# A 64-expert mixture-of-experts kernel: one eighth of a one-block expert's second product as plain fp32, second-block transposes into other banks, one-pass ranks and routing table

## The chip, the cores and the metric

The kernel runs on one core of a Trainium2 chip. The metric is the device time of one execution in microseconds (us). Its engines are TensorE (PE; its weight loads are listed apart as PEld), VectorE (DVE), ScalarE (ACT), GpSimd (POOL) and SyncE (SP, which here only issues transfers). They run side by side and wait for each other through semaphores.

## The reference

One layer of a hybrid model over 2048 tokens of width 1024: a normed and modulated input goes through a spatial-gating branch and a gated linear-attention branch, whose merged output is added to the residual. Then a second norm and a mixture of experts:

```
hn2 = modulate(rmsnorm(h, g_norm2), sh2, sc2)
pg = softmax(t @ wrg + brg); p_top, g_idx = top_k(pg, 1)          # 8 groups
l_top, e_local = top_k(le[g_idx], 2)                              # 8 experts in each
gate = p_top * softmax(l_top)                                     # two experts per token
hblk = silu(xblk @ w1[e]) * (xblk @ w3[e])                        # [128,1024] @ [1024,512] twice
y    = hblk @ w2[e]                                               # [128,512] @ [512,1024]
out  = rmsnorm(h + g2 * segment_sum(y * gate), g_final)
```

Tokens are sorted by expert into blocks of 128. With these inputs 57 of the 64 experts fill one block and seven fill two.

## The kernel before

**Precision.** All products are to be as good as fp32. A matrix is split into a high part `hi`, rounded to the format fp32r, and a rest `lo`; `split_w` (lines 79 to 81) does it with one ACT copy (L80) and one DVE subtraction (L81). A product is then three fp32r matmuls (`mm3`, L84 to L86): hi by hi, hi by lo, lo by hi. Products of F32 operands are left to the engine's plain fp32, which the built program lists as one matmul and the trace as two instructions.

**Routing (phase D, up to line 1151).** A loop over sixteen tiles of 128 tokens, last tile first, mixes 48 large products per iteration (`pmx`, the output projection), the norm, the router's logits (`pl`) and, for a tile some iterations back, its routing: `g_route` picks the experts (one-hot `oh`, sum `ot`), `g_rank` ranks the tokens of an expert by a product with a triangle of ones (`prk`: one product with `ot`, one with the running counts `coh`), and builds `what` (token number and gate at the expert's column) and `at` (one-hot of the rank). `d_tab` adds four products at^T what into `slots`, the table of tokens and gates by rank and expert. After the loop the last two tiles go through without other work beside them, and DVE takes indices `idx` and gates `gate` from `slots`.

**Experts (from line 1160).** Each expert has twelve weight tiles of 128 x 1024 (eight for the first two products, four for the second), each two halves of 512 columns: 24 halves, 16 of `up` and 8 of `down`. SP loads tiles into a ring of 28; a load waits until its ring place has been read for the last time. `need` issues the split of a half LA = 4 halves ahead of its product, into a ring of eight pairs `wh`, `wl`. `block` runs over the halves of `up` (into the two `pa` banks) or `down` (into the two `py` banks). The order on each engine is that in which the code is written: `up(e+1)` comes ahead of `down(e)`, then `yevac` of `py` (DVE, two instructions L1218) and the scatter-add (POOL). Within `down`, at its fifth half, the next-but-one expert's rows are transposed (`xprep`, L1196, into `tpe`) and split (`xhe`, `xle`); at its seventh half the gated rows are transposed (`htr`, L1204, into `th`) for the next `down`; they are split (`hsplit`, L1208 and L1209) at the fifth half of the next `up`.

Whether an expert has a second block is known only at run time: `up` and `down` are each written twice, under If (two blocks) and Else (one), by `both`. In the two-block form `up` first transposes the second block's rows `xq` into `py`, runs its products three halves behind into `tpe`, and `down` runs the second block into `pa`, which DVE then evacuates inside the branch (L1218 on `pa`).

Of the kernel before, what the change touches and what calls it, by code (L numbers as in the profile page):

```python
# [8 lines left out]
F32 = mybir.dt.float32  # L9
F32R = mybir.dt.float32r  # L10
# [3 lines left out]
AF = mybir.ActivationFunctionType  # L14
# [3 lines left out]
P = 128  # L18
# [12 lines left out]
def kernel(ctx: ExitStack, tc: tile.TileContext, a: dict, out: bass.AP):  # L31
# [16 lines left out]
    def pt(tag, shape, name):  # L48
        return psp.tile(list(shape), F32, name=name, tag=tag, bufs=NB[tag])
# [29 lines left out]
    def split_w(raw, hi, lo):  # L79
        act.activation(hi, raw, AF.Copy)  # L80
        vec.tensor_tensor(lo, raw, hi.bitcast(F32), op=OP.subtract)  # L81
# [761 lines left out]
    p1s.close()  # L843


    coh = const.tile([P, NE], F32, name="coh")
    vec.memset(coh, 0.0)
    zero = const.tile([P, 1], F32, name="zero")
    vec.memset(zero, 0.0)
    es = ExitStack()  # L850
    wk = es.enter_context(tc.tile_pool(name="p1d", bufs=1))
    bc = [wk.tile([P, D], F32, name=f"bc{i}") for i in range(2)]
    wr = wk.tile([P, KD, G + NE], F32, name="wr")
    br = wk.tile([P, G + NE], F32, name="br")
# [92 lines left out]
    def g_route(ti, rs=None):  # L947
        L = wk.tile([P, G + NE], F32, name="L", tag="L", bufs=2)
        if rs is None:
            vec.tensor_tensor(L, PL[ti], br, op=OP.add)  # L950
            yield
        else:
            vec.scalar_tensor_tensor(L, PL[ti], rs, br2, op0=OP.mult, op1=OP.add)
            yield
        gm, gi, gif = sm("gm", 8), sm("gi", 8, U32), sm("gif")
        vec.max(gm, L[:, 0:8])
        yield
        vec.max_index(gi, gm, L[:, 0:8])
        yield
        vec.tensor_copy(gif, gi[:, 0:1])  # L960
        yield
        nm, se, eg = sm("nm"), sm("se"), sm("eg", 8)
        og, mk = sm("og", 8), wk.tile([P, G, EG], F32, name="mk", tag="mk", bufs=2)
        vec.tensor_scalar(og, iota[:, 0:8], gif, None, op0=OP.is_equal)
        yield
        vec.tensor_scalar(nm, gm[:, 0:1], -1.0, None, op0=OP.mult)
        yield
        act.activation(eg, L[:, 0:8], AF.Exp, bias=nm, accum_out=se)
        vec.tensor_tensor(mk, L[:, 8:72].rearrange("p (g e) -> p g e", g=G),
                          og[:, :, None].to_broadcast([P, G, EG]), op=OP.mult)  # L970
        yield
        le = sm("le", 8)
        vec.tensor_reduce(le, mk.rearrange("p g e -> p e g"), axis=AX.X, op=OP.add)
        yield
        m1, i1, f = sm("m1", 8), sm("i1", 8, U32), sm("f", 2)
        vec.max(m1, le)
        yield
        vec.max_index(i1, m1, le)
        yield
        vec.tensor_copy(f[:, 0:1], i1[:, 0:1])  # L980
        yield
        o1, le2 = sm("o1", 8), sm("le2", 8)
        vec.tensor_scalar(o1, iota[:, 0:8], f[:, 0:1], None, op0=OP.is_equal)
        yield
        vec.scalar_tensor_tensor(le2, o1, -3.0e38, le, op0=OP.mult, op1=OP.add)
        yield
        m2, i2 = sm("m2", 8), sm("i2", 8, U32)
        vec.max(m2, le2)
        yield
        vec.max_index(i2, m2, le2)  # L990
        yield
        vec.tensor_copy(f[:, 1:2], i2[:, 0:1])
        yield
        df, e2, ef = sm("df"), sm("e2"), sm("ef", 2)
        vec.tensor_tensor(df, m2[:, 0:1], m1[:, 0:1], op=OP.subtract)
        yield
        act.activation(e2, df, AF.Exp)
        vec.scalar_tensor_tensor(ef, gif.to_broadcast([P, 2]), 8.0, f, op0=OP.mult, op1=OP.add)
        yield
        oh = wk.tile([P, 2, NE], F32, name="oh", tag="oh", bufs=2)  # L1000
        vec.tensor_tensor(oh, iota[:, None, :].to_broadcast([P, 2, NE]), ef[:, :, None].to_broadcast([P, 2, NE]),
                          op=OP.is_equal)
        yield
        ot = wk.tile([P, NE], F32, name="ot", tag="ot", bufs=2)
        vec.tensor_tensor(ot, oh[:, 0], oh[:, 1], op=OP.add)
        yield
        RT[ti] = e2, se, ot, oh, ef

    def g_rank(ti, *more_):
        e2, se, ot, oh, ef = RT[ti]  # L1010
        dn = sm("dn")
        prk = pt("aux", [P, NE], "prk")
        pe.matmul(prk, low, ot, start=True, stop=False)
        for m in more_:
            pe.matmul(prk, ones, m, start=False, stop=False)
        pe.matmul(prk, ones, coh, start=False, stop=True)
        pair = const.tile([P, 2, 2], F32, name="pair", tag="pair", bufs=3)
        pool.tensor_copy(pair[:, :, 0], tok[:, ti:ti + 1].to_broadcast([P, 2]))
        what = wk.tile([P, 2, 2, NE], F32, name="what", tag="what", bufs=2)
        act.activation(what[:, :, 0], oh, AF.Copy, scale=tok1[:, ti:ti + 1])  # L1020
        vec.scalar_tensor_tensor(dn, e2, 1.0, se, op0=OP.add, op1=OP.mult)
        yield
        vec.reciprocal(pair[:, 0, 1:2], dn)
        yield
        vec.tensor_tensor(pair[:, 1, 1:2], pair[:, 0, 1:2], e2, op=OP.mult)
        yield
        for i in range(2):
            act.activation(what[:, i, 1], oh[:, i], AF.Copy, scale=pair[:, i, 1:2])
        rk, at = sm("rk", 2), wk.tile([P, 2, 2 * P], F32, name="at", tag="at", bufs=2)
        ri = const.tile([P, 2], I32, name="ri", tag="ri", bufs=3)  # L1030
        prod = wk.tile([P, 2, NE], F32, name="prod", tag="prod", bufs=2)
        vec.tensor_tensor(prod, oh, prk[:, None, :].to_broadcast([P, 2, NE]), op=OP.mult)
        yield
        vec.tensor_tensor(coh, coh, ot, op=OP.add)
        yield
        vec.tensor_reduce(rk, prod, axis=AX.X, op=OP.add)
        yield
        for i in range(2):
            vec.tensor_scalar(at[:, i], pos, rk[:, i:i + 1], None, op0=OP.is_equal)
            yield  # L1040
        vec.scalar_tensor_tensor(ri, ef, float(S), rk, op0=OP.mult, op1=OP.add)
        yield
        SC[ti], TB[ti] = (ri, pair), (at, what)
# [32 lines left out]
    for it in range(NT):  # L1076
# [1 line left out]
        if it > 1:  # L1078
            d_x(ti)
        if it == 2:  # L1080
            slots = pt("mm", [P, 2, 2, NE], "slots")
            vec.memset(slots, 0.0)
        if it == 1:
            d_split(ti - 1)
# [62 lines left out]
    none = wk.tile([P, 2, NE], F32, name="none")  # L1147
    vec.tensor_scalar(none, slots[:, :, 0], 0.0, off, op0=OP.is_equal, op1=OP.mult)
    vec.scalar_tensor_tensor(idx.rearrange("p (b e) -> p b e", b=2), slots[:, :, 0], -1.0, none, op0=OP.add, op1=OP.add)
    vec.tensor_copy(gate.rearrange("p (b e) -> p b e", b=2), slots[:, :, 1])  # L1150
    es.close()


# [20 lines left out]
    PA, TP, PY, TH = ([psp.tile([P, 512], F32, name=f"{n}{i}") for i in range(2)] for n in ("pa", "tpe", "py", "th"))  # L1174
    four = lambda t: t.rearrange("p (c n) -> p c n", c=4)
    pc = TH[1][:, 0:NE]
    pe.matmul(pc, ones, coh, start=True, stop=True)
    ci_ = wk.tile([1, NE], I32, name="ci_")
    vec.tensor_scalar(ci_, pc[0:1], float(P - 1), None, op0=OP.add)
    vec.tensor_scalar(nblk, ci_, 7, None, op0=OP.logical_shift_right)  # L1180
# [4 lines left out]
    xhl = [wk.tile([P, KD, P], F32R, name=n) for n in ("xhe", "xle")]  # L1185
    hx = [wk.tile([P, KF, P], F32R, name=n) for n in ("hhe", "hle")]
    hx2 = [wk.tile([P, KF, P], F32R, name=n) for n in ("hh2", "hl2")]
    sh = wk.tile([P, F], F32, name="she")
    sh2 = [wk.tile([P, F], F32, name=f"sh2{i}") for i in range(2)]
    y1 = wk.tile([P, D], F32, name="y1")  # L1190
# [15 lines left out]
    def hsplit(th, hx):  # L1206
        hh, hl = hx
        act.activation(hh, four(th), AF.Copy)  # L1208
        vec.tensor_tensor(hl, four(th), hh.bitcast(F32), op=OP.subtract)  # L1209

    def glu(pa, sh):
# [18 lines left out]
    hpos = {v: p for p, v in enumerate(hseq)}  # L1230
    nsp = 0

    def need(p):
        nonlocal nsp
        while nsp <= min(p, len(hseq) - 1):
            e, k, i = hseq[nsp]
            split_w(W[e, k][:, i * 512:(i + 1) * 512], *ring[nsp % R])
            nsp += 1

    def both(two, one):  # L1240
# [13 lines left out]

        return [t.rearrange("p (k n) -> p k n", k=KD) for t in (xgr[e % 3], xqr[e % 2])]

    def block(base, n, outs, hls, at):

        for q in range(n + (LAG if len(outs) > 1 else 0)):
            if q < n:  # L1260
                need(base + q + LA)
                if q in at:
                    at[q]()
            for j, (o, hl) in enumerate(zip(outs, hls)):
                p = q - j * LAG
                if 0 <= p < n:
                    mms(o[p % 2], hl, p // 2, p % 2, n // 2, ring[(base + p) % R])

    def more(e):
# [44 lines left out]
    def up(e):  # L1314

        at = {4: lambda: hsplit(TH[0], hx)} if e else {}
        base = hpos[e, 0, 0]

        def two():
            xprep(xq[e % 2], rows2(e), PY)  # L1320
            block(base, 2 * KD, (PA, TP), (xhl, rows2(e)), at)
            glu(PA, sh)
            glu(TP, sh2[e % 2])

        def one():
            block(base, 2 * KD, (PA,), (xhl,), at)
            glu(PA, sh)

        g = both(two, one)
        with tc.If(NB_[e] > 1, preferred_fallthrough_block=False) as f:  # L1330
            next(g)
        with f.Else():
            next(g, None)

    def down(e):
# [13 lines left out]
            scat(y2, col(idx, NE + e))  # L1349

        def one():
            block(base, 2 * KF, (PY,), (hx,), at)

        g = both(two, one)
        with tc.If(NB_[e] > 1, preferred_fallthrough_block=False) as f:
# [119 lines left out]
```

## Time and profile before

| | us |
|---|---|
| three runs: lowest, median, highest | 2403.30, 2412.09, 2412.42 |
| profiled execution, its own time | 2410.06 |
| its span | 2408.4 |
| PE busy in the span | 2259.7 (94%) |
| DVE busy | 1932.1 (80%) |
| ACT busy | 1437.3 (60%) |
| POOL busy | 739.2 (31%) |

The profiled execution's time lies 2.0 us below the median of the runs. The mean granted clock is 0.969. Phase D spans about 780 to 1030 us, the experts about 1030 to 2330 us. A busy share averages over stages with different limits, so the views below are read stage by stage. A matmul's duration overlaps the next one's: what a product costs is the distance between starts.

### The profile page before, as it was taken

The page shows a single profiled execution, that of the slowest core. Times are in us where ns is not written, and L with a number is a line of the kernel's source. Part 1 is how long each engine was busy: PE and PEld are TensorE (multiplying, and loading weights), DVE is VectorE, ACT ScalarE, POOL GpSimd, SP SyncE. Part 2 cuts the span into 40 slices and gives each one's busy share as a digit, 9 for nine tenths or more (in the row PEclk, how much of TensorE's full clock was granted, in tenths as well). Part 3 has the DMA queues.
Part 4 walks back from the last instruction along what each step waited for, and adds up shares of the span by engine and source line. Part 5 has one row for each costly group of instructions (what it writes and reads, how often), then busy time and mean ns, then how long its engine had stood idle before and what let it go on. Part 6 is the DMA issues. An engine that isn't in the chain of part 4 may idle for free.

```text
span 2408.4 us, 40084 instructions
## 1 busy us (share of the span) xinstructions
PE 2259.7 (94%) x11932; PEld 1860.0 (77%) x11932; DVE 1932.1 (80%) x4302; ACT 1437.3 (60%) x2731; POOL 739.2 (31%) x602
## 2 busy tenths in 40 slices
PE   8999999989999899899999999999999999999990
PEld 3888888977777788778777888888777788888870
DVE  4556665657786888789887899999686699999986
ACT  3544444432332222378676788888575688888873
POOL 1123311146673122237431222323131132322220
PEclk9899999989999999989999999999999999999995
DMA  7333322356675654589997899999996799999947
GB/s 274 105 107 106 121 92 97 109 170 210 219 241 175 227 210 159 184 323 374 323 310 259 292 377 372 365 352 348 325 327 194 223 360 373 368 358 363 360 140 296
DMA packets 193220, 613.42 MB, mean 255 GB/s; under 512 B 36557, under 2 KB 36685, under 8 KB 192854
## 3 DMA queue, kind: packets, MB, share of 16 engines
q1 hardware_dynamic: 152358, 516.56, 59.0%
q0 software_dynamic: 38048, 87.95, 12.4%
q10 hardware_dynamic: 2448, 4.46, 0.5%
q8 instruction: 178, 2.92, 0.5%
q14 instruction: 188, 1.54, 0.2%
HBM read 547.42 MB, written 102.28 MB: 270 GB/s over the span
## 4 chain that ended last, share of the span: by engine, by line
PE 35%; DVE 11%; DMA 6%; issue 5%; ACT 1%; DVEq 0%; another core or an unknown queue 0%; SPq 0%; POOLq 0%; ACTq 0%; POOL 0%
DVE wl L81 9%; PE pa L84 7%; PE pa L86 7%; PE pa L85 7%; DMA we<-in_w_e_dram 3%; PE py L84 2%; PE py L85 2%; PE py L86 2%; DMA accD<-y,idx 2%; PE tpe L1196 1%; PE tpe L85 1%; PE tpe L84 1%; PE tpe L86 1%; DVE y L1218 1%; ACT wh L80 1%
## 5 line engine op out<-in xcount | busy, mean ns | idle before, releaser
L81 DVE TENSOR_TENSOR wl<-we,wh 128x512 fp32r<-128x512 f32 x1536 | 967.6, 732 | 82.5 <-ACT wh L80 76.2
L80 ACT ACTIVATE wh<-we 128x512 fp32r<-128x512 f32 x1536 | 892.9, 630 | 146.3 <-DVE wl L81 46.3
L84 PE MATMUL pa<-wh,xhe 128*128 128x512 f32 x1024 | 404.2, 395 | 9.5 <-ACT wh L80 7.5
L1221 POOL DMA_INDIRECT accD<-y,idx x71 | 245.7, 3460 | 525.0 <-DVE y L1218 440.5
L86 PE MATMUL pa<-wh,xle 128*128 128x512 f32 x1024 | 400.4, 391 | 0.0
L85 PE MATMUL pa<-wl,xhe 128*128 128x512 f32 x1024 | 399.9, 391 | 0.0
L84 PEld LDWEIGHTS pa<-wh,xhe 128*128 128x128 f32 x1024 | 192.6, 188 | 69.9 <-issue 28.6
L86 PEld LDWEIGHTS pa<-wh,xle 128*128 128x128 f32 x1024 | 192.6, 188 | 41.0
L1163 POOL DMA_INDIRECT xg<-hnD,idx x64 | 96.5, 1508 | 410.7 <-DVE wl L81 124.9
L85 PEld LDWEIGHTS pa<-wl,xhe 128*128 128x128 f32 x1024 | 192.8, 188 | 37.6
L84 PE MATMUL py<-wh,hhe 128*128 128x512 f32 x512 | 213.5, 417 | 6.7 <-ACT wh L80 6.2
L86 PE MATMUL py<-wh,hle 128*128 128x512 f32 x512 | 202.7, 396 | 1.5 <-issue 1.3
L85 PE MATMUL py<-wl,hhe 128*128 128x512 f32 x512 | 201.1, 393 | 2.9 <-DVE wl L81 2.9
L86 PEld LDWEIGHTS py<-wh,hle 128*128 128x128 f32 x512 | 97.0, 190 | 25.3 <-issue 3.1
L351 POOL TENSOR_SCALAR sc<-sc,dec 64x128 f32<-64x128 f32 x140 | 111.1, 793 | 17.8 <-PE po L683 6.4
L84 PEld LDWEIGHTS py<-wh,hhe 128*128 128x128 f32 x512 | 97.4, 190 | 24.5 <-issue 6.1
L85 PEld LDWEIGHTS py<-wl,hhe 128*128 128x128 f32 x512 | 97.7, 191 | 16.0
L1071 POOL DMA_INDIRECT tabD<-pair,ri x32 | 70.0, 2189 | 91.4 <-DMA tabD<-pair,ri 59.0
L1218 DVE SCALAR_TENSOR_TENSOR y<-py,gate,g2b 128x512 f32<-128x512 f32 x128 | 93.0, 791 | 4.0 <-PE py L86 3.9
L86 PE MATMUL pmx<-hi,mld 128*128 128x512 f32 x224 | 89.0, 397 | 6.1 <-DVE mld L81 6.1
L84 PE MATMUL pmx<-hi,mhd 128*128 128x512 f32 x224 | 91.9, 410 | 1.7 <-ACT mhd L80 1.7
L85 PE MATMUL pmx<-lo,mhd 128*128 128x512 f32 x224 | 88.0, 393 | 0.0
(417 smaller groups left out, 4651.2 us busy)
## 6 DMA issues: line engine op xcount, KB each, us to landing
we<-in_w_e_dram SPq DMA_DIRECT2D x765, 512.0 KB, 9.9
wt<-in_w_modB_dram SPq DMA_DIRECT2D x32, 512.0 KB, 5.7
kve<-kveD SPq DMA_DIRECT2D x48, 256.0 KB, 5.5
wt<-in_w_modA_dram SPq DMA_DIRECT2D x16, 512.0 KB, 7.5
x<-in_x_dram SPq DMA_DIRECT2D x16, 512.0 KB, 3.8
xD<-xf POOLq DMA_DIRECT2D x32, 256.0 KB, 3.1
mfd<-mxD SPq DMA_DIRECT2D x16, 512.0 KB
xd<-in_x_dram SPq DMA_DIRECT2D x16, 512.0 KB, 5.0
```

Source lines behind the costliest of these rows:

```text
L80: act.activation(hi, raw, AF.Copy)
L81: vec.tensor_tensor(lo, raw, hi.bitcast(F32), op=OP.subtract)
L84: pe.matmul(o, lh, wh, start=start, stop=False)
L85: pe.matmul(o, lh, wl, start=False, stop=False)
L86: pe.matmul(o, ll, wh, start=False, stop=stop)
L351: pool.tensor_scalar(s1[64:128, hs], s0[64:128, hs], dec[64:128, ci, h:h + 1], None, op0=OP.mult)
L1071: pool.indirect_dma_start(out=tabD, out_offset=bass.IndirectOffsetOnAxis(ap=ri[:, i:i + 1], axis=0), in_=pair[:, i], in_offset=None)
L1163: pool.indirect_dma_start(out=x, out_offset=None, in_=hnD, in_offset=bass.IndirectOffsetOnAxis(ap=ix, axis=0), bounds_check=S - 1, oob_is_ ...
L1196: pe.transpose(four(tp[c // 4])[:, c % 4], x[:, c * P:(c + 1) * P], ident)
L1218: vec.scalar_tensor_tensor(y[:, c], py[i], gt, g2b[:, c], op0=OP.mult, op1=OP.mult)
L1221: pool.indirect_dma_start(out=accD, out_offset=bass.IndirectOffsetOnAxis(ap=ix, axis=0), in_=y, in_offset=None, bounds_check=S - 1, oob_is ...
```

## The change

1. **Routing.** `ot`, `coh`, `what`, `at` and the two constant matrices (copied into `lor`) become fp32r, so `prk` and the table are single fp32r matmuls. Ones, token numbers and ranks are whole numbers; the gate is not, and is carried as `gh` + `gl` in two columns: `what` and `slots` grow from 2 to 3 x 64 columns, DVE adds the two after the loop.
2. **Second block.** `xprep` of the second block's rows goes into `tpe` instead of `py`.
3. **One-block `down`.** The last of its eight halves (position `raw`) is not split. Its product is one plain fp32 matmul of the raw weight half with `hf`, an unsplit copy of the last 128 columns of the gated rows, which ACT makes beside `hhe` in the space of a constant no longer used. The two-block form keeps all splits.

```diff
+    lor = wk.tile([P, 2, P], F32R, name="lor")
+    vec.tensor_copy(lor.rearrange("p t c -> p (t c)"), cst[:, 5 * P:7 * P])
+    lowr, onesr = lor[:, 0], lor[:, 1]
...
-        pe.matmul(prk, low, ot, start=True, stop=False)
+        pe.matmul(prk, lowr, ot, start=True, stop=False)
...
-        what = wk.tile([P, 2, 2, NE], F32, name="what", tag="what", bufs=2)
+        what = wk.tile([P, 2, 3, NE], F32R, name="what", tag="what", bufs=2)
...
+        gh, gl = wk.tile([P, 2], F32R, name="gh", tag="gh", bufs=2), sm("gl", 2)
+        act.activation(gh, pair[:, :, 1], AF.Copy)
+        vec.tensor_tensor(gl, pair[:, :, 1], gh.bitcast(F32), op=OP.subtract)
+        yield
         for i in range(2):
-            act.activation(what[:, i, 1], oh[:, i], AF.Copy, scale=pair[:, i, 1:2])
-        rk, at = sm("rk", 2), wk.tile([P, 2, 2 * P], F32, name="at", tag="at", bufs=2)
+            act.activation(what[:, i, 1], oh[:, i], AF.Copy, scale=gh[:, i:i + 1].bitcast(F32))
+            act.activation(what[:, i, 2], oh[:, i], AF.Copy, scale=gl[:, i:i + 1])
+        rk, at = sm("rk", 2), wk.tile([P, 2, 2 * P], F32R, name="at", tag="at", bufs=2)
...
-    vec.tensor_copy(gate.rearrange("p (b e) -> p b e", b=2), slots[:, :, 1])
+    ghi = wk.tile([P, 2, NE], F32, name="ghi")
+    vec.tensor_copy(ghi, slots[:, :, 1])
+    vec.tensor_tensor(gate.rearrange("p (b e) -> p b e", b=2), ghi, slots[:, :, 2], op=OP.add)
...
+    hf = tri_f
...
         act.activation(hh, four(th), AF.Copy)
+        if th is TH[0]:
+            act.activation(hf, four(th)[:, KF - 1], AF.Copy)
...
-            split_w(W[e, k][:, i * 512:(i + 1) * 512], *ring[nsp % R])
+            if nsp != raw:
+                split_w(W[e, k][:, i * 512:(i + 1) * 512], *ring[nsp % R])
             nsp += 1
...
-                if 0 <= p < n:
+                if base + p == raw:
+                    e, k, i = hseq[raw]
+                    pe.matmul(o[i], hf, W[e, k][:, i * 512:(i + 1) * 512], start=False, stop=True)
+                elif 0 <= p < n:
                     mms(o[p % 2], hl, p // 2, p % 2, n // 2, ring[(base + p) % R])
...
-            xprep(xq[e % 2], rows2(e), PY)
+            xprep(xq[e % 2], rows2(e), TP)
...
-            block(base, 2 * KF, (PY,), (hx,), at)
+            block(base, 2 * KF, (PY,), (hx,), at, base + 2 * KF - 1)
```

PE, the end of `down` in its one-block form, before (`py` and `th` are banks, `wh`/`wl` the split half, `she` the gated rows; the branch ends the form):

```order
L1204 MATMUL th_11188<-cst,she 128x128 x4
L84 MATMUL py_11186<-wh_11219,hhe 128x512
L85 MATMUL py_11186<-wl_11220,hhe 128x512
L86 MATMUL py_11186<-wh_11219,hle 128x512
L84 MATMUL py_11187<-wh_11221,hhe 128x512
L85 MATMUL py_11187<-wl_11222,hhe 128x512
L86 MATMUL py_11187<-wh_11221,hle 128x512
L1355 UNCONDITIONAL_BRANCH
```

and now (`cst` holds `hf`, `we` is the raw tile):

```order
L1216 MATMUL th_11288<-cst,she 128x128 x4
L84 MATMUL py_11286<-wh_11319,hhe 128x512
L85 MATMUL py_11286<-wl_11320,hhe 128x512
L86 MATMUL py_11286<-wh_11319,hle 128x512
L1283 MATMUL py_11287<-we_11234,cst 128x512
L1373 UNCONDITIONAL_BRANCH
```

One instruction (two in a trace) stands where three stood; nothing else on PE moves there. DVE in the same form, before:

```order
L81 TENSOR_TENSOR wl_11220<-we_11136,wh_11219 128x512
L81 TENSOR_TENSOR wl_11222<-we_11136,wh_11221 128x512
L81 TENSOR_TENSOR wl_11208<-we_11138,wh_11207 128x512
L1200 TENSOR_TENSOR xle<-tpe_11184,xhe 128x512
L1200 TENSOR_TENSOR xle<-tpe_11185,xhe 128x512
L81 TENSOR_TENSOR wl_11210<-we_11138,wh_11209 128x512
L81 TENSOR_TENSOR wl_11212<-we_11140,wh_11211 128x512
L81 TENSOR_TENSOR wl_11214<-we_11140,wh_11213 128x512
L1355 UNCONDITIONAL_BRANCH
```

and now:

```order
L81 TENSOR_TENSOR wl_11320<-we_11234,wh_11319 128x512
L81 TENSOR_TENSOR wl_11308<-we_11236,wh_11307 128x512
L1212 TENSOR_TENSOR xle<-tpe_11284,xhe 128x512
L1212 TENSOR_TENSOR xle<-tpe_11285,xhe 128x512
L81 TENSOR_TENSOR wl_11310<-we_11236,wh_11309 128x512
L81 TENSOR_TENSOR wl_11312<-we_11238,wh_11311 128x512
L81 TENSOR_TENSOR wl_11314<-we_11238,wh_11313 128x512
L1373 UNCONDITIONAL_BRANCH
```

The split of the last half (`wl_11222` before) is gone; the splits of the next `up` move one place forward. The routing loop on PE, as the difference of two places in one iteration:

```order
-L1013 MATMUL prk<-ot,cst 128x64
-L1016 MATMUL prk<-coh,cst 128x64
+L1017 MATMUL prk<-ot,lor 128x64
+L1020 MATMUL prk<-coh,lor 128x64
-L1064 MATMUL slots<-what,at 128x128 x4
+L1073 MATMUL slots<-what,at 128x192 x4
```

The places in the order stay; the products are now of fp32r operands and the table's are 192 columns wide.

## Rows read from the trace of the kernel before

**Rows 1.** Busy time by stretch: from and to, length, then busy time and instructions of PE, PEld, DVE, ACT and POOL, granted clock, share of the DMA engines, GB/s. The first stretch holds one-block experts alone, the second the routing loop.

```profile
1378.00:1687.00 309.00, 305.19 (x1428) 248.89 (x1427) 309.00 (x512) 267.72 (x474) 91.98 (x35) 1.00 0.99 363
830.00:1003.00 173.00, 173.00 (x971) 149.49 (x971) 141.53 (x569) 49.78 (x125) 45.12 (x59) 1.00 0.46 169
```

**Rows 2.** The timeline around the end of one `down` in that stretch: start, duration, engine, line, output and inputs, count, and in brackets idle time before it.

```profile
1499.21 3.17 DVE L81 TENSOR_TENSOR wl<-we,wh 128x512 fp32r<-128x512 f32 x5
...
1500.51 1.03 PE L1196 MATMUL tpe<-cst,xg 128*128 128x128 f32 x8
...
1501.30 0.47 PE L84 MATMUL py<-wh,hhe 128*128 128x512 f32 x1
...
1504.12 0.39 PE L85 MATMUL py<-wl,hhe 128*128 128x512 f32 x1
...
1504.35 0.40 PE L86 MATMUL py<-wh,hle 128*128 128x512 f32 x1
...
1504.89 0.19 PEld L84 LDWEIGHTS pa<-wh,xhe 128*128 128x128 f32 x1 [0.58 <-issue]
1504.92 0.47 PE L84 MATMUL pa<-wh,xhe 128*128 128x512 f32 x1 [0.18 <-ACT wh L80]
...
1505.23 1.48 DVE L1218 SCALAR_TENSOR_TENSOR y<-py,gate,g2b 128x512 f32<-128x512 f32 x2
1505.23 0.39 PE L85 MATMUL pa<-wl,xhe 128*128 128x512 f32 x1
```

**Rows 3.** The same place one expert later.

```profile
1522.47 0.40 PE L86 MATMUL py<-wh,hle 128*128 128x512 f32 x1
...
1523.09 0.47 PE L84 MATMUL pa<-wh,xhe 128*128 128x512 f32 x1 [0.22 <-ACT wh L80]
...
1523.37 1.49 DVE L1218 SCALAR_TENSOR_TENSOR y<-py,gate,g2b 128x512 f32<-128x512 f32 x2
```

**Rows 4.** The timeline of DVE, the last split ahead of the y at 1505.23.

```profile
1504.63 0.75 DVE L81 TENSOR_TENSOR wl<-we,wh 128x512 fp32r<-128x512 f32 x1
```

**Rows 5.** Waits of PE's weight loads over the expert stage (1030 to 2330): waiting group, releaser, us in total, times, longest.

```profile
PEld pa L84 <- issue: 28.6, 48, 0.7
```

**Rows 6.** The timeline of PE in the routing stage, plain fp32 products of 512 columns (L740: two products, four instructions) and what follows.

```profile
838.96 1.88 PE L740 MATMUL pm<-macc,cst 128*128 128x512 f32 x4
...
840.28 0.80 PE L84 MATMUL pmx<-hi,mhd 128*128 128x512 f32 x1
...
840.91 0.40 PE L85 MATMUL pmx<-lo,mhd 128*128 128x512 f32 x1
```

**Rows 7.** Groups of PE instructions over the expert stage: busy us, mean ns of one, idle us before them and what ended it. All transposes of second blocks.

```profile
L1196 PE MATMUL py<-cst,xq 128*128 128x128 f32 x56 | 9.0, 284 | 9.6 <-issue 7.5 <-DVE y L1218 2.2
```

**Rows 8.** The timeline at the head of one two-block `up`.

```profile
1248.01 0.40 PE L86 MATMUL py<-wh,hle 128*128 128x512 f32 x1
1249.04 1.41 DVE L1218 SCALAR_TENSOR_TENSOR y<-py,gate,g2b 128x512 f32<-128x512 f32 x2
...
1249.90 1.27 PE L1196 MATMUL py<-cst,xq 128*128 128x128 f32 x8 [1.49 <-issue]
...
1250.92 0.48 PE L84 MATMUL pa<-wh,xhe 128*128 128x512 f32 x1
```

**Rows 9.** The timeline of PE in one iteration of the routing loop.

```profile
891.25 0.33 PE L1013 MATMUL prk<-ot,cst 128*128 128x64 f32 x2
891.41 0.39 PE L1016 MATMUL prk<-coh,cst 128*128 128x64 f32 x2
891.63 1.96 PE L945 MATMUL pl<-wr,ht 128*128 128x72 f32 x16
...
898.99 1.06 PE L1064 MATMUL slots<-what,at 128*128 128x128 f32 x8
899.88 1.04 PE L934 MATMUL tpd<-cst,hn 128*128 128x128 f32 x8
...
906.26 0.33 PE L1013 MATMUL prk<-ot,cst 128*128 128x64 f32 x2
```

**Rows 10.** Groups of the routing loop (830 to 1003): the ACT instruction that writes a gate column of `what`, and the one-column DVE product beside it.

```profile
L1028 ACT ACTIVATE what<-oh,pair 128x64 f32<-128x64 f32 x24 | 7.1, 341 | 70.6 <-DVE pair L1023 70.6
...
L1025 DVE TENSOR_TENSOR pair<-pair,e 128x1 f32<-128x1 f32 x12 | 1.9, 159 | 0.4
```

**Rows 11.** The timeline after the loop: the first and the last products of the ranks of the last two tiles, their table, and DVE's first read of it.

```profile
1018.57 0.69 PE L1013 MATMUL prk<-ot,cst 128*128 128x64 f32 x2 [4.75 <-DVE ot L1005]
...
1020.33 0.63 PE L1016 MATMUL prk<-coh,cst 128*128 128x64 f32 x2
...
1022.48 3.75 PE L1064 MATMUL slots<-what,at 128*128 128x128 f32 x16 [1.51 <-DVE at L1039]
...
1026.27 0.35 DVE L1148 TENSOR_SCALAR none<-slots,off 128x128 f32<-128x128 f32 x1 [3.01 <-PE slots L1064]
```

**Rows 12.** The DMA view of 1380 to 1680 (all traffic; the weight loads, their KB and median us from issue to landing) and SP's waits there.

```profile
DMA packets 32746, 109.03 MB, mean 363 GB/s; under 512 B 6268, under 2 KB 6268, under 8 KB 32677
...
we<-in_w_e_dram SPq DMA_DIRECT2D x192, 512.0 KB, 11.3
...
SPq L613 <- DMA we<-in_w_e_dram: 117.5, 109, 3.1
SPq L613 <- DVE wl L81: 99.7, 120, 2.0
```

More of the change, by code (lines that the diff above doesn't have):

```diff
@@ L843 @@
     p1s.close()
-    coh = const.tile([P, NE], F32, name="coh")
-    vec.memset(coh, 0.0)
+    coh = const.tile([P, NE], F32R, name="coh")
+    cohf = coh.bitcast(F32)
+    vec.tensor_scalar(coh, cst[:, 0:NE], 0.0, None, op0=OP.mult)
     zero = const.tile([P, 1], F32, name="zero")
@@ L1003, in g_route @@
         yield
-        ot = wk.tile([P, NE], F32, name="ot", tag="ot", bufs=2)
+        ot = wk.tile([P, NE], F32R, name="ot", tag="ot", bufs=2)
         vec.tensor_tensor(ot, oh[:, 0], oh[:, 1], op=OP.add)
@@ L1012, in g_rank @@
         prk = pt("aux", [P, NE], "prk")
-        pe.matmul(prk, low, ot, start=True, stop=False)
+        pe.matmul(prk, lowr, ot, start=True, stop=False)
         for m in more_:
-            pe.matmul(prk, ones, m, start=False, stop=False)
-        pe.matmul(prk, ones, coh, start=False, stop=True)
+            pe.matmul(prk, onesr, m, start=False, stop=False)
+        pe.matmul(prk, onesr, coh, start=False, stop=True)
         pair = const.tile([P, 2, 2], F32, name="pair", tag="pair", bufs=3)
         pool.tensor_copy(pair[:, :, 0], tok[:, ti:ti + 1].to_broadcast([P, 2]))
-        what = wk.tile([P, 2, 2, NE], F32, name="what", tag="what", bufs=2)
+        what = wk.tile([P, 2, 3, NE], F32R, name="what", tag="what", bufs=2)
         act.activation(what[:, :, 0], oh, AF.Copy, scale=tok1[:, ti:ti + 1])
@@ L1033, in g_rank @@
         yield
-        vec.tensor_tensor(coh, coh, ot, op=OP.add)
+        vec.tensor_tensor(coh, cohf, ot.bitcast(F32), op=OP.add)
         yield
@@ L1080 @@
         if it == 2:
-            slots = pt("mm", [P, 2, 2, NE], "slots")
+            slots = pt("mm", [P, 2, 3, NE], "slots")
             vec.memset(slots, 0.0)
@@ L1176 @@
     pc = TH[1][:, 0:NE]
-    pe.matmul(pc, ones, coh, start=True, stop=True)
+    pe.matmul(pc, ones, cohf, start=True, stop=True)
     ci_ = wk.tile([1, NE], I32, name="ci_")
@@ L1231, with need @@
     nsp = 0
-    def need(p):
+    def need(p, raw=None):
         nonlocal nsp
@@ L1255, in rows2, with block @@
         return [t.rearrange("p (k n) -> p k n", k=KD) for t in (xgr[e % 3], xqr[e % 2])]
-    def block(base, n, outs, hls, at):
+    def block(base, n, outs, hls, at, raw=None):
         for q in range(n + (LAG if len(outs) > 1 else 0)):
             if q < n:
-                need(base + q + LA)
+                need(base + q + LA, raw)
                 if q in at:
```

## The prediction

> **What bounds the kernel now.** I read busy time by stretch first, since the change touches stages with different limits. In a stretch of one-block experts DVE is busy for all of its 309.00 us, in 512 instructions, so one every 0.604 us; PE is busy for 305.19 us [rows 1]. The timeline gives the period: one y starts at 1505.23, the next at 1523.37, 18.14 us later [rows 2, 3]. In it DVE has 30 instructions (24 weight splits, two xle, one hle, one she, two y), and 30 x 0.604 = 18.1. So DVE bounds a one-block expert, although PE's bar looks as full.
>
> The timeline also shows where PE gives the difference back. Products of the same kind start 0.23 us apart (1504.12, 1504.35). At the head of the next up the step is 0.57 (1504.35 to 1504.92), and one expert later 0.62 (1522.47 to 1523.09) [rows 2, 3]. The step behind it is 0.31 (1504.92 to 1505.23) in place of 0.23: a refill. The profile calls the wait "issue". The row of DVE says more: its last split began at 1504.63, so the one ahead of it, 0.604 earlier, with its duration of 0.75, ended at 1504.78, and PE's weight load begins at 1504.89 [rows 2, 4]. I read the gap as a wait for DVE: PE's first write to a pa bank waits on DVE's count, which in the one-block form has to reach the same place as in the two-block form, where DVE reads pa behind its last splits. PE alone would need 18.14 - 0.37 - 0.08, on average of the stops: **17.70 us**. The waits count 48 such stops over the expert stage [rows 5]; going through them in the timeline I put 41 behind one-block experts. In the rest DVE is not full.
>
> The routing loop is the opposite: PE is busy for 173.00 of 173.00 us and DVE for 141.53 [rows 1], at one iteration per 15.01 us (891.25 to 906.26) [rows 9]. What PE is spared there is gained.
>
> **One-block experts.** The change takes one split of 0.604 from DVE and one from ACT, which is not full (267.72 of 309.00) [rows 1]. DVE then has 29 instructions, 29 x 0.604 = 17.5 us. ACT gets a small copy instead; at most 0.34, the duration of a smaller one in routing [rows 10], it is under the split it replaces. On PE three fp32r steps of 0.23, 0.68 in all, become one plain fp32 product. The trace has such products of 512 columns: from the first of four L740 instructions (838.96) to the second product behind them (840.91) it takes 1.95 us, less the one fp32r step of 0.23 is 1.72 for two, **0.86 each**, entering and leaving fp32 included [rows 6]. That adds 0.18. An upper bound is one refill more, 0.08 as behind the present stop, so 0.26; below 0.86 nothing in the trace points. PE's period becomes 17.70 + 0.18 = 17.88, above DVE's 17.5: PE is now the bound, with DVE 0.3 to 0.4 us ahead of it per expert, which is what keeps the stop from coming back. The sum: 41 stops of 0.45 go, **-18.5**; 57 one-block experts pay 0.18, **+10.2** (bounds +10 to +15).
>
> [...]
>
> What is queued behind: the raw half is read by PE and no longer by DVE. DVE's fourth split from 1499.21 was the one of this half, over by about 1501.8; a product in its place on PE ends at about 1504.8 [rows 2]. So one of twelve weight tiles comes free 3 us later, and SP, which issues in order, holds back what stands behind it. A load takes 11.3 us from issue to landing at one per 1.56 us (192 in 300 us) [rows 12], so some seven are on their way and the bus stays fed: nothing.
>
> **Second blocks.** The eight transposes of second rows wait for DVE's y on py, the bank that they write. In one case y starts at 1249.04 and lasts to 1250.45; the transposes begin 1.89 us after the last product (1248.01 to 1249.90) in place of 0.23, and take 1.02 us to the next product in place of the 0.79 that undisturbed ones take (1500.51 to 1501.30) [rows 2, 8]. That is 1.66 + 0.23 = 1.89 us. The seven cases show PE idle for 9.6 us [rows 7]. Idle time counts from a product's end, 0.17 behind the start that the next would have had (a duration of 0.40 at steps of 0.23), so 7 x 0.17 = 1.2 come on top, and 7 x 0.23 = 1.6 for the slower transposes: 12.4. Bank tpe was last read by DVE's xle, two in a row behind the five splits from 1499.21 in an ordinary down and over before its last product, so the moved transposes find it free. What is late next would be xq: y ends at 1250.45, the first xq split, no longer than the 0.75 of a weight split [rows 4], by 1251.2. The next up would start at 1248.01 + 0.23 + 0.79 = 1249.03, and its products with xq four halves of 0.69 later, at 1251.8: in time. **-12.4** (bounds -9.6 to -12.5).
>
> **Routing loop.** Ranks take 0.38 us (891.25 to 891.63), the table 0.89 for eight instructions, 0.11 each (898.99 to 899.88) [rows 9]. The trace of before has no fp32r product below 256 columns. From below, the nearest row is an instruction of the table: 0.11 us, with its weight load. Four such make the table 0.45, two make the ranks 0.22: 0.60 per iteration. From above, plain fp32's rate: 192 of 512 columns of 0.86 is 0.32, four make 1.29, and the ranks stay as they are: 0.40 more. I take the lower price, since fp32r products of 512 columns here run at 0.23, so the format itself costs one pass. DVE and ACT get more work per tile: gl 0.16, a wait of one ACT step (0.34) ahead of it, and on ACT three more instructions of 0.34 [rows 10]; both have room (DVE 31 us, ACT 123 us idle in 173) [rows 1], and the table's product comes 7 us behind the ranks. Twelve iterations: **-7.3** (bounds -8 to +5).
>
> **Tail and setup.** After the loop the ranks and the table of the last two tiles stand on the path: DVE waits 3.01 us for the table [rows 11]. Eight rank instructions take 1.76 us (1018.57 to 1020.33), 0.22 each; ten become five, -1.1. Sixteen table instructions in 3.75 become eight, -1.9. The gate needs one more DVE instruction, at 0.35 as its neighbour [rows 11]; the larger setup and the wait for gh add some 0.6. **-2.0** (bounds -3 to +3, the last with fp32's rate).
>
> **Sum** against the profiled execution's 2410.06: -18.5 + 10.2 - 12.4 - 7.3 - 2.0 = **-30.0**, so 2380 us; that execution lies 2.0 below the median of the three runs, of which I give half back: **2381**.
>
> **Rivals.**
>
> *1. fp32r is slow when narrow.* If under 256 columns it goes at plain fp32's rate, the loop gains nothing: +4.8 in place of -7.3, and the tail loses its gain of 2. 2381 + 12 + 2 = **2395**. For it: no row shows a narrow one. Against it: the wide ones' rate. 0.17.
>
> *2. The transfers bound one-block experts.* All DMA engines are at 0.99, at 363 GB/s, in that stretch [rows 1]; 192 tiles in 300 us are 18.75 us for twelve, more than the 18.14 in which they are used [rows 12]. Then the net 8.3 us of these experts is lost: **2389**. [...] Against the rival: the ring holds 28 tiles, 2.3 experts. Over 300 us, 198.5 tiles are used and 192 come, 6.5 from the ring; at 17.88 us it is 9.3. SP still waits 120 times for DVE to free a place [rows 12], so the ring is full for half of the stretch, and the two-block experts fill it again. 0.10.
>
> *3. The stop is PE's own.* "issue" could be a branch or code that PE fetches. Then the 18.5 us stay: **2400**, rounded up. Against it: a step of 0.23 at the same place where DVE is not full, and the 0.1 us between DVE's split and PE's load. 0.06.
>
> *4. Slower: the late tile empties the transfer queue.* Place: SP, once per expert. If its hold of 3 us leaves the DMA engines idle for x us, the ring loses x per expert and is empty within one saturated stretch; after that each expert takes 18.75 + x. Over 41 experts, with half of the ring's 42 us (28 tiles at 18.14 / 12) spent first, some 20, x = 2 costs 41 x 2 - 20 = 62, so **2443**; it makes the kernel slower than before from about x = 1.2 on. Against it: seven loads under way last 11 us. 0.03.
>
> *5. The moved transposes wait elsewhere*, for xle or at the product that needs xq: the 12.4 go, **2393**. Against it: the margins above. 0.06.
>
> **How the numbers follow.** My forecast has 0.58: what the five rivals leave. The range: the bounds of its terms give 2377 to 2400 around it (fp32 +5, second blocks +3, tail and loop up to the first rival's), rivals 1, 2, 3 and 5 lie inside or on the edge. Below it, three runs of one kernel spread over 9 us (2403.30 to 2412.42), and a DVE with time to spare may also shorten other stops of PE: **2367 to 2400**. This kernel's measurement can tell about 0.5%, 12 us, from no change, so faster ends at 2400. Forecast and rivals 1, 2 and 5 (0.91) lie below it, rival 3 (0.06) on it, two of them together above it, for which I take 0.06 off: faster 0.85, same 0.11, slower 0.04 (rival 4 and 0.01 for what I don't see).
>
> **What would show it.** In the changed profile: the step at the head of up is 0.23 and DVE idles 0.3 to 0.4 us per expert; y to y is 17.9 (18.15 speaks for rival 2 or 3, more for rival 4); the fp32 half is two instructions 0.43 apart; the second blocks' transposes begin 0.23 behind the last product; iterations of the routing loop take 14.4 us (15.4 for rival 1). The forecast is wrong if PE waits in one-block experts for ACT's wh with a load as releaser, or if the refill appears behind every fp32 product.

## The result: 2388.49 us, 0.9% faster; PE's waits for its own program took back a part of the gain

| | before | changed |
|---|---|---|
| median of five runs (range), us | 2410.49 (2403.30 to 2412.42) | 2388.49 (2380.69 to 2390.06) |
| profiled execution, us (span) | 2410.06 (2408.4) | 2388.58 (2386.9) |
| ratio of the runs, 95% interval | | 0.9912 (0.9895 to 0.9929) |

The medians differ by 22.0 us, where the forecast was 30 less than the profiled execution before (2381).

The places that the prediction's terms name look as they were drawn. The two stretches of [rows 1] after the change, with the same columns:

```profile
830.00:1003.00 173.00, 167.94 (x916) 143.97 (x916) 148.18 (x601) 60.97 (x170) 51.34 (x61) 1.00 0.50 183
1378.00:1687.00 309.00, 307.45 (x1427) 249.24 (x1426) 303.60 (x498) 259.77 (x479) 66.19 (x35) 1.00 1.00 360
```

DVE is no longer full in the one-block stretch, and PE is no longer full in the routing loop. In the one-block stretch PE is not quite full either (307.45 of 309.00 us); what holds it there is part of what follows. The end of a one-block down, answering to [rows 2, 3]:

```profile
1521.60 0.39 PE L86 MATMUL py<-wh,hle 128*128 128x512 f32 x1
1521.83 1.02 PE L1283 MATMUL py<-we,cst 128*128 128x512 f32 x2
1522.35 0.73 PE L84 MATMUL pa<-wh,xhe 128*128 128x512 f32 x1
1522.72 0.74 DVE L1232 SCALAR_TENSOR_TENSOR y<-py,gate,g2b 128x512 f32<-128x512 f32 x1
1522.91 0.39 PE L85 MATMUL pa<-wl,xhe 128*128 128x512 f32 x1
```

From the first fp32 instruction (1521.83) to the second product behind it (1522.91) it takes 1.08 us; less one step of 0.23 this is 0.85 to 0.86, the price taken from [rows 6]. No stop follows, and the heads of up lie 17.89 us apart, where 17.88 was forecast. The head of a two-block up, answering to [rows 8]:

```profile
1240.19 1.02 PE L1283 MATMUL py<-we,cst 128*128 128x512 f32 x2
1241.05 1.04 PE L1208 MATMUL tpe<-cst,xq 128*128 128x128 f32 x8
1241.07 1.40 DVE L1232 SCALAR_TENSOR_TENSOR y<-py,gate,g2b 128x512 f32<-128x512 f32 x2
1241.84 0.48 PE L84 MATMUL pa<-wh,xhe 128*128 128x512 f32 x1
```

The transposes follow the product at once, beside y, and take 0.79 us. PE in one iteration of the routing loop, answering to [rows 9], and then the table of the last two tiles, answering to [rows 11]:

```profile
891.56 0.19 PE L1017 MATMUL prk<-ot,lor 128*128 128x64 f32 x1
891.59 0.27 PE L1020 MATMUL prk<-coh,lor 128*128 128x64 f32 x1
891.70 1.99 PE L949 MATMUL pl<-wr,ht 128*128 128x72 f32 x16
...
899.08 0.58 PE L1073 MATMUL slots<-what,at 128*128 128x192 f32 x4
899.50 1.04 PE L938 MATMUL tpd<-cst,hn 128*128 128x128 f32 x8
...
905.88 0.19 PE L1017 MATMUL prk<-ot,lor 128*128 128x64 f32 x1
...
1016.63 2.09 PE L1073 MATMUL slots<-what,at 128*128 128x192 f32 x8 [1.54 <-DVE at L1048]
```

Ranks take 0.14 and the table 0.42 us, an iteration 14.32 (forecast 14.4). Narrow fp32r products do not go at plain fp32's rate: 192 columns take 0.105 us, where that rate gave 0.32. The last table takes 2.09 us, where it took 3.75 in [rows 11]. PE's waits over the expert stage (1030 to 2300), answering to [rows 5], show what is left:

```profile
PE th L1216 <- issue: 5.7, 2, 4.4
PE py L85 <- DVE wl L81: 3.6, 1, 3.6
PE py L86 <- issue: 2.9, 2, 2.7
PE tpe L1208 <- issue: 1.3, 2, 0.8
PE pa L84 <- DVE y L1232: 1.3, 5, 0.3
PE tpe L1208 <- DVE she L1227: 0.2, 1, 0.2
```

The stops at pa's head are gone, but there are long ones in places where the prediction has none, the three longest of 4.4, 3.6 and 2.7 us. The second, put down to DVE, in the timeline of PE:

```profile
1282.38 0.48 PE L84 MATMUL py<-wh,hhe 128*128 128x512 f32 x1
...
1286.47 0.59 PE L85 MATMUL py<-wl,hhe 128*128 128x512 f32 x1 [3.62 <-DVE wl L81]
```

DVE's splits ran from 1283.90 on, one every 0.6 us, so the half that PE needed was there two microseconds earlier. All three (1208, 1282, 1342 us) lie just behind the branch into a two-block down. Two DMA queues bring instructions, q8 in packets of 16384 bytes (178 in the whole trace, 2.92 MB) and q14 in packets of 8192 (187, 1.53 MB). From the start of the first packet of q8 (39.4 us) to that of the 46th (989.6), where PE's program has no branch, PE has 5655 products, 5656 weight loads and 186 waits that stand by themselves: 255.5 instructions to each of 45 packets (255.2 in the trace of before). The DMA view of 1282.4 to 1286.5 has one packet of each; that of q8 began at 1283.93 and took 0.92:

```profile
q8 instruction: 1, 0.02, 1.4%
...
q14 instruction: 1, 0.01, 0.5%
```

PE goes on 1.62 us after the end of the q8 packet. The same holds in all twelve traces of this document: at each of the 29 stops of more than 1 us between the first up and the last (leaving out second-block transposes that wait for y), PE goes on 1.2 to 1.8 us after the end of a q8 packet; from the end of the last q14 packet it is anything from 0.0 to 24 us. So these are waits for PE's instructions, and q8 is the queue that brings them.

A stop also costs more than its length. PE stood idle for 3.6 us, and then its granted clock was 0.50 for 6 us, with products 0.43 us apart in place of 0.23:

```profile
1286.40:1292.40 6.00, 5.93 (x14) 4.46 (x14) 0.00 (x0) 0.00 (x0) 0.00 (x0) 0.50 0.61 247
```

Behind the stop of 4.4 us the clock was at that level for 3.4 us (1347.1 to 1350.5); behind the one of 2.7 us it stayed at 1.00.

From the first pa product of the first up to that of the last the trace shows 1287.41 us before and 1270.92 after: -16.5, where the sum had -20.7. The last expert has one more, of 2.0 us of idle time at 2315.

### The profile page after: what moved, and what is told of

It reads as the page before. It is cut to its first block, busy times and chain, and to the rows that moved or that the text cites. A ratio compares the mean times of both kernels' runs of the same rounds, so it can differ in the third digit from the quotient of the medians.

```text
span 2386.9 us, 39665 instructions
## 1 busy us (share of the span) xinstructions
PE 2245.7 (94%) x11778; PEld 1840.1 (77%) x11778; DVE 1901.8 (80%) x4263; ACT 1415.1 (59%) x2786; POOL 636.9 (27%) x602
## 3 DMA queue, kind: packets, MB, share of 16 engines
q8 instruction: 178, 2.92, 0.5%
q14 instruction: 187, 1.53, 0.2%
## 4 chain that ended last, share of the span: by engine, by line
PE 51%; DMA 3%; issue 2%; DVE 1%; another core or an unknown queue 0%; SPq 0%; POOLq 0%; DVEq 0%; ACT 0%; POOL 0%
PE pa L84 10%; PE pa L86 10%; PE pa L85 10%; PE py L86 4%; PE py L84 4%; PE py L85 4%; PE tpe L1208 3%; PE py L1283 2%; DMA accD<-y,idx 2%; PE th L1216 1%; PE tpe L85 1%; PE tpe L84 1%; PE tpe L86 1%; DMA hf<-accD 1%; DVE hf L1428 0%
## 5 line engine op out<-in xcount | busy, mean ns | idle before, releaser
L81 DVE TENSOR_TENSOR wl<-we,wh 128x512 fp32r<-128x512 f32 x1479 | 921.0, 686 | 88.4 <-ACT wh L80 84.9
L80 ACT ACTIVATE wh<-we 128x512 fp32r<-128x512 f32 x1479 | 850.4, 632 | 140.0 <-DVE wl L81 50.2
L84 PE MATMUL pa<-wh,xhe 128*128 128x512 f32 x1024 | 418.7, 409 | 1.3 <-DVE y L1232 1.3
L1235 POOL DMA_INDIRECT accD<-y,idx x71 | 181.3, 2554 | 553.7 <-DVE y L1232 448.6
L1174 POOL DMA_INDIRECT xg<-hnD,idx x64 | 75.9, 1186 | 474.6 <-DVE wl L81 147.4
L84 PE MATMUL py<-wh,hhe 128*128 128x512 f32 x455 | 191.3, 420 | 4.9 <-ACT wh L80 4.8
L86 PE MATMUL py<-wh,hle 128*128 128x512 f32 x455 | 180.7, 397 | 5.5 <-issue 4.8
L85 PE MATMUL py<-wl,hhe 128*128 128x512 f32 x455 | 179.3, 394 | 3.6 <-DVE wl L81 3.6
L86 PEld LDWEIGHTS py<-wh,hle 128*128 128x128 f32 x455 | 86.6, 190 | 24.4 <-issue 4.5
L1211 ACT ACTIVATE xhe<-tpe 128x512 fp32r<-128x512 f32 x128 | 69.9, 594 | 51.3 <-PE tpe L1208 49.1
L85 PEld LDWEIGHTS py<-wl,hhe 128*128 128x128 f32 x455 | 87.4, 192 | 13.5
L1212 DVE TENSOR_TENSOR xle<-tpe,xhe 128x512 fp32r<-128x512 f32 x128 | 82.9, 686 | 14.4 <-ACT xhe L1211 12.8
```

Source lines behind the costliest of these rows:

```text
L84: pe.matmul(o, lh, wh, start=start, stop=False)
L85: pe.matmul(o, lh, wl, start=False, stop=False)
L86: pe.matmul(o, ll, wh, start=False, stop=stop)
L1174: pool.indirect_dma_start(out=x, out_offset=None, in_=hnD, in_offset=bass.IndirectOffsetOnAxis(ap=ix, axis=0), bounds_check=S - 1, oob_is_ ...
L1211: act.activation(xh[:, qs], four(tp[q]), AF.Copy)
L1212: vec.tensor_tensor(xl[:, qs], four(tp[q]), xh[:, qs].bitcast(F32), op=OP.subtract)
```

## The experiments

Each time is the median of four to ten runs; the kernel before gave 2404.91 to 2408.0 beside them. "Skipped" are small products put into a branch that is never taken, counted in PE instructions. "Expert stage" is the length just defined, in the one profiled execution of each run.

| run | median, us | ratio (95%) | expert stage, us |
|---|---|---|---|
| part 3 alone | 2383.85 | 0.9906 (0.9881 to 0.9931) | 1261.22 |
| part 2 alone | 2389.93 | 0.9933 (0.9907 to 0.9960) | 1267.10 |
| part 1 alone | 2413.02 | 1.0018 (1.0005 to 1.0031) | 1297.76 |
| changed, 128 skipped | 2365.75 | 0.9828 (0.9803 to 0.9853) | 1251.13 |
| changed, 4 skipped | 2390.11 | 0.9925 (0.9896 to 0.9955) | 1275.81 |
| changed, 64 skipped | 2367.06 | 0.9830 (0.9792 to 0.9868) | 1251.80 |
| before, 128 skipped | 2393.50 | 0.9950 (0.9929 to 0.9972) | 1275.49 |
| changed, split kept | 2401.35 | 0.9981 (0.9967 to 0.9995) | 1284.17 |
| changed, 248 skipped | 2389.24 | 0.9928 (0.9904 to 0.9952) | 1275.43 |
| every second, 128 skipped | 2374.72 | 0.9872 (0.9851 to 0.9893) | 1259.01 |

**One part at a time.** The kernel before with one part of the change.

```diff
-            block(base, 2 * KF, (PY,), (hx,), at)
+            block(base, 2 * KF, (PY,), (hx,), at, base + 2 * KF - 1)
```

> The kernel before with part 3 alone: the last half of a one-block down as one plain fp32 product of the raw weights. By the prediction's terms: 41 stops of 0.45 us gone, 57 products 0.18 us dearer, -8.3 us against the kernel before, period of a one-block expert 17.9 us. Rival (the 7 us that the whole change fell short were lost in this part): about -1 us, with waits for weight loads or an idle SP in one-block experts. What I can't place beforehand: stops of PE with no releaser (the profile says issue) inside two-block downs; they sum to 10.3 us in the trace of before and 13.9 in that of the change up to the last expert, so +-4 us on top.

24 us faster. The period is 17.89, and the expert stage has none of the long stops. So this part had no loss, and something else went with it.

```diff
-            xprep(xq[e % 2], rows2(e), PY)
+            xprep(xq[e % 2], rows2(e), TP)
```

> The kernel before with part 2 alone: second blocks' transposes into tpe. No PE instruction is added or taken away, so PE's program stays where it was. Theory (the shortfall is PE waiting for its program, which depends on where the program's blocks lie): the four long stops of before stay at the same places (second halves of two-block downs 4 and 6, transposes late in the expert stage) and the time is -12.4 us +-1. Rival (a stop that the waits on DVE covered is uncovered when they go): new stops in two-block downs, and -6 to -9 us.

18 us faster. The premise was wrong: PE's program got instructions more (its trace has 476 waits that stand by themselves, where that of before has 462), and the stops of before did not stay; one of 2.3 us came at 1713 us. Neither theory's list of stops fits, so this run does not decide between them.

```diff
-        pe.matmul(prk, low, ot, start=True, stop=False)
+        pe.matmul(prk, lowr, ot, start=True, stop=False)
...
-        what = wk.tile([P, 2, 2, NE], F32, name="what", tag="what", bufs=2)
+        what = wk.tile([P, 2, 3, NE], F32R, name="what", tag="what", bufs=2)
```

> The kernel before with part 1 alone: ranks and table as fp32r. Terms of the prediction: -9.3 us; in the changed kernel's trace the routing stage gains 8.9 (iteration 14.3 us, 0.7 less, of which 3 us are given back at two places where PE then waits for DVE). If the rest of the shortfall sat here: -2 to -5. PE's program gets shorter by some hundred instructions, so by the theory on PE's program the stops in the experts move, up to +-5 us.

5 us slower, though the experts' code is that of before and nothing in it was touched: their stage took 1297.76 us against 1287.41. Its waits over the expert stage:

```profile
PE th L1215 <- issue: 6.1, 2, 4.4
PE py L85 <- DVE wl L81: 5.0, 2, 3.8
...
PE py L86 <- issue: 3.8, 1, 3.8
PE tpe L1207 <- issue: 1.4, 2, 0.7
```

Work that ends before 1030 us changed stops at 1208, 1288 and 1349 us. What it did to the experts is to make PE's program in front of them shorter; that this is the cause is tested next.

**The place of PE's program.** The changed kernel with products in a branch that is never taken, ahead of the experts; `n_products` is 1, 16, 32 or 62, each of them four instructions, and the branch itself adds seven:

```diff
     need(LA - 1)
+    n = nc.values_load(most, engines=[mybir.EngineType.PE], min_val=0, max_val=S // P,
+                       skip_runtime_bounds_check_because=BOUND)
+    with tc.If(n > S // P - 1, preferred_fallthrough_block=False):
+        for _ in range(n_products):
+            pe.matmul(TH[0][:, 0:2], ident, ones[:, 0:2], start=True, stop=True)
```

> The changed kernel with 32 small fp32 products (128 PE instructions with their weight loads) ahead of the experts in a branch that is never taken, at a place where PE waits for rows anyway: the work is the same, PE's program behind it lies 128 instructions further. Theory (stops inside experts are PE waiting for its program, placed by where blocks of the program end): the stops named issue (now at 1208, 1282, 1342, 1727, 2314 and 2324 us, 15 us in sum) come at other places or not, and the time moves by 2 to 10 us either way. Rival (they belong to what the code does there): the same stops, the time within 1.5 us of the changed kernel's (the branch itself may cost 0.5).

23 us faster than the changed kernel without it, more than was expected. All of PE's waits from 1030 to 2280 us:

```profile
PE pa L84 <- DVE y L1232: 1.3, 5, 0.3
PE tpe L1208 <- DVE she L1227: 0.2, 1, 0.2
```

Every one-block expert takes 17.89 us and not one long stop is left before the last expert.

> As the run with 128 instructions of padding ahead of the experts, but with one small product (4 instructions) in the branch that is never taken. If the place of PE's program sets the stops, 4 instructions and the branch's own few hardly move it: the stops of the changed kernel stay (1208, 1282, 1342, 1727 us and their lengths of 1.5 to 4.4 us) and the time is 2386 to 2391 us. Rival (the branch itself, not the distance, took the stops away): 2364 to 2368 us and no stops, as with 128.

The time stayed; the stops did not quite: the branch and four instructions, eleven in all, moved them by a few products, to the first transposes behind the branch and once into an up:

```profile
PE th L1216 <- issue: 13.5, 3, 4.6
PE pa L84 <- ACT wh L80: 2.0, 1, 2.0
```

So it is not the branch that takes them away.

> 16 small products (64 instructions) in the branch that is never taken. If the place of PE's program sets the stops: some of them stay or others come, a time between the changed kernel's 2388 and the padded one's 2366 us, or above. Rival (the branch itself): 2366 us, as with 128.

No long stop and 2367.06 us, not what was expected: between 4 and 64 instructions there is a place from which they vanish, and this run alone would fit the rival too.

> The changed kernel with 62 small products (248 instructions, 255 with the branch's own) in the branch that is never taken. PE's program comes in transfers of 16384 bytes, which are 256 instructions of 64 bytes. Theory (the stops depend on where such a piece ends): a shift of 255 is nearly a whole piece, so the changed kernel's stops come back at the same places of the program (two-block downs at 1208, 1282, 1342 us, of 3 to 4.6 us, and 1.7 at 1727) and the time is about 2388 us. Rival (more padding or a longer jump simply takes stops away): 2366 us and none, as with 64 and 128.

They are back, in the same order and nearly the same sizes, and so is the time, 2389.24. One of 1.2 us at 1583 is new, and the expert stage is 4.5 us longer than in the changed kernel. Its waits from 1035 to 2310 us, and the third expert's stop in the timeline of PE:

```profile
PE th L1216 <- issue: 9.2, 3, 4.2
PE py L86 <- issue: 3.2, 1, 3.2
```

```profile
1291.56 0.38 PE L1216 MATMUL th<-cst,sh 128*128 128x128 f32 x2
1295.93 0.38 PE L1216 MATMUL th<-cst,sh 128*128 128x128 f32 x2 [3.99 <-issue]
```

With the branch's own seven, a shift of 11 leaves the stops, 71 or 135 take them away, 255 brings them back. This is what would come of places that repeat with a packet of q8, some 256 instructions; other periods were not tested. Together with the packets of q8 this shows that PE waits there for its own program: the place behind a branch, the packet that ends 1.2 to 1.8 us before PE goes on, and a shift of 255 that changes little all fit. What makes a packet come late at such a place is not shown. One stop was up to 4.6 us, and all of them with the clock behind them 20 us of an execution.

> The kernel before with the same 128 instructions in a branch that is never taken ahead of the experts. If stops go with the place of PE's program, those of before (3.3 us at 1730, 4.6 at 1901, 1.7 at 2135, 1.6 at 2171, in all some 12 us with what follows) come elsewhere: 2396 to 2415 us. If a branch at this place, or this distance, always takes them away: 2396. Beside the padded changed kernel (2366) it shows what the change is worth without them: the terms gave 30 us.

11 us faster by padding alone, a little below both forecasts. What is left of its waits from 1030 to 2305 us is what the change removes:

```profile
PE pa L84 <- ACT wh L80: 7.4, 37, 0.3
PE py L1196 <- issue: 5.9, 4, 1.6
PE py L1196 <- DVE y L1218: 3.7, 3, 1.5
```

With both kernels free of stops the expert stage is 1275.49 before and 1251.13 after, **24.4 us less**, and the medians are 27.7 us apart (2393.50, 2365.75). In these two profiled executions the routing loop's first ranks come at 804.0 and 813.1 us, so the 9 us that routing gains do not show in their own times (2389.24 and 2365.09); why runs differ ahead of the loop is taken up at the end.

Part 3 alone has no stops of PE's program either, so the 24.4 us divide: 14.3 from the padded kernel before to part 3 alone (1261.22), and 10.1 from there to the padded changed kernel, which is what part 2 is worth beside part 3.

**Who sets the one-block stop.** DVE's and ACT's split of the raw half is made again and not used:

```diff
-            if nsp != raw:
+            if True:
                 split_w(W[e, k][:, i * 512:(i + 1) * 512], *ring[nsp % R])
```

> The changed kernel, but the split of the last half of a one-block down is still made by ACT and DVE and not used. PE's instructions are all the same. Theory (DVE's 30 instructions set the 18.15 us of a one-block expert, and PE's stop at the head of up is a wait for DVE): period 18.15 us again, the stop back at about 0.27 us less than the 0.45 it was, and 41 x 0.27 = 11 us slower than the changed kernel, about 2399. Rival (the stop went because PE's program changed at that place): 17.89 as in the changed kernel, same time.

13 us slower than the changed kernel, and the stretch 1930 to 2290 has DVE full again:

```profile
1930.00:2290.00 360.00, 359.07 (x1647) 286.59 (x1646) 360.00 (x596) 314.22 (x576) 107.22 (x39) 1.00 0.99 361
```

```profile
2067.22 1.02 PE L1283 MATMUL py<-we,cst 128*128 128x512 f32 x2
2068.30 0.47 PE L84 MATMUL pa<-wh,xhe 128*128 128x512 f32 x1
2068.61 0.39 PE L85 MATMUL pa<-wl,xhe 128*128 128x512 f32 x1
```

From the first fp32 instruction to pa now 1.08 us, where it was 0.52 (1521.83 to 1522.35); the period is 18.16. PE's matmuls are the same, one for one, so the stop at pa comes from the split. Of its two halves it is DVE's: in 38 of the 41 stops of before, PE's weight load begins 0.115 to 0.117 us behind the end of a DVE instruction, and 0.06 to 0.11 behind one of ACT, which is not full. The long stops in two-block downs came at the same instructions of PE's program as in the changed kernel (1204, 1277 and 1337 us), though all times around them had moved.

**A balance between PE and DVE.** The plain product in every second one-block expert, padded by 128:

```diff
-            block(base, 2 * KF, (PY,), (hx,), at, base + 2 * KF - 1)
+            block(base, 2 * KF, (PY,), (hx,), at, base + 2 * KF - 1 if e % 2 else None)
```

> The padded changed kernel (128) with the plain fp32 product in every second one-block expert only; the others keep all 24 splits. PE's mean period is 17.70 + 0.09 = 17.79, DVE's 29.5 x 0.604 = 17.82. Theory (PE needs 17.70 and 0.18 more for a plain product, DVE 0.604 per instruction, and the buffers of four halves let one expert lend the next): 17.82 on the mean of two, 0.07 less than 17.887, 3 to 4 us faster than with every expert where no stops of PE's program come in, about 2362. Rival (no lending: every second expert pays DVE's 18.1): mean period 18.0, 6 us slower, about 2372. Stops of PE's program can add up to 15 us either way; the period is read from the trace.

Neither. Three y in a row of its timeline:

```profile
1499.73 1.41 DVE L1232 SCALAR_TENSOR_TENSOR y<-py,gate,g2b 128x512 f32<-128x512 f32 x2
1517.34 1.40 DVE L1232 SCALAR_TENSOR_TENSOR y<-py,gate,g2b 128x512 f32<-128x512 f32 x2
1535.50 1.40 DVE L1232 SCALAR_TENSOR_TENSOR y<-py,gate,g2b 128x512 f32<-128x512 f32 x2
```

17.61 and 18.16, 35.77 for two: 17.885 on the mean, the same as with every expert. Two experts' 59 instructions on DVE are 35.64, so one expert does lend to the next, but 0.13 us of the pair are lost, just what was to be gained. Stops of PE's program came with it (3.0 us at 1866 us, two of 1.0 and 0.8), since every second expert has two instructions more. The expert stage is 7.9 us longer than in the padded changed kernel: 6.3 us more idle time of PE, and 3.4 us at half clock behind the longest stop. That is most of the 9 us between the medians.

## Why the prediction was right, and where its size was off

- **One-block experts** (-18.5, +10.2): the mechanism is shown, by the period of 17.89, the fp32 product of 0.86, and the stop that comes back with DVE's thirtieth instruction. The count was low: with PE's own stops out of the way, 45 experts of the padded kernel before have the stop, not 41; the four at 2119 to 2194 us had hidden it behind stops of PE's program. Part 3 alone against the padded kernel before is -14.3 in the expert stage, where the terms give -8.3, or -10.1 with 45. Of the other 4, 3.1 are second blocks: PE's idle time before their transposes falls from 9.6 to 6.6 us with part 3 alone, since four of the seven waits for y are 0.7 us in place of 1.4.
- **Second blocks** (-12.4): waits and slow transposes are gone at all seven. Part 2 alone is -8.4 in the expert stage against the padded kernel before, with some 4 us of stops of PE's program of its own in it; beside part 3 it is worth 10.1, as part 3 has taken 3.1 of the waits already.
- **Routing and tail** (-7.3, -2.0): from the first ranks of the loop to the first up the trace shows 221.7 us before and 212.7 after, -9.0. The loop gained more (0.70 an iteration, 0.61 forecast), and 3 us of it went into two places where PE, now earlier, waits for DVE: 2.66 us for br at 830, 2.40 for the ranks' input at 998.
- **Rivals.** 1 falls with the 0.105 us of a narrow product, 3 with the kept split, as far as the head of up goes (code that PE fetches, which it named, is what stops PE elsewhere), 5 with the seven heads. 2 and 4 ask for one-block experts held by transfers: with the DMA engines at 1.00 in that stretch the period is 17.89, in the padded kernel for all of them.
- **The step that failed** is the first line of the sum, which took the 2410.06 us of the profiled execution as if all in it that the terms don't name would stay. Its trace had four long stops at 1730, 1901, 2135 and 2171 us that no term names. They are PE waiting for its program, and an edit that changes the number of PE's instructions deals them anew. Against the padded kernels they cost 1287.41 - 1275.49 = 11.9 us before and 1270.92 - 1251.13 = 19.8 after. Of the 19.8, 13.5 are idle time of PE, and some 4, by an estimate from the steps of 0.43 and 0.23, are the 9.4 us at half clock behind two of them; the rest I did not separate.
- **How near the number came is partly luck.** Between the two profiled executions the kernel is 21.5 us faster. That is 24.4 less in the expert stage without stops (forecast 20.7) and 9.0 less in routing and tail (forecast 9.3); against it stand 7.9 for the stops, 2.0 for a longer last expert, with its own stop in it, and 1.9 by which the loop began later. The terms were worth 33 and not 30, and this covered part of what the stops took.

## What to carry to other kernels

This long program with branches has a lottery in it: the place of PE's instructions decided over up to 23 us (2388.49 against 2365.75), more than any one part of the change (14.3 us). When two versions of such a program differ in their instruction count, shift each by some 64 and some 128 skipped instructions before judging an edit by a per cent; the changed kernel padded by 128 or 64, at 2365.75 and 2367.06 us, is the fastest of all tried. And a stop that a profile calls "issue" behind a branch, on an engine whose inputs are ready, is to be looked up among the instruction packets before it is put down to the work. So is a stop that the profile puts down to another engine which had long been done, as the one of 3.6 us here.

## What was not expected of the hardware

Before the first edited instruction the two traces already differ: the changed kernel's was 1.9 us later at the loop's first ranks, having been 5 us earlier at 699 us. In 756 to 761 us it shows PE at half clock where the trace of before has the full one (first row after, second before):

```profile
756.00:761.00 5.00, 5.00 (x21) 3.27 (x18) 0.65 (x4) 1.14 (x8) 0.00 (x0) 0.50 0.00 0
756.00:761.00 5.00, 5.00 (x33) 3.54 (x33) 2.62 (x7) 1.14 (x8) 0.00 (x0) 1.00 0.00 0
```

The granted clock of such a stage differs from execution to execution, though nothing in it was changed: over the twelve traces the loop's first ranks come between 802.4 and 817.5 us. How much of the some 10 us between runs of one kernel is that, I did not separate. Only stage lengths within a trace told effects of a few microseconds apart.
